# A planned hybrid-layer kernel on one core: room behind GpSimd operations and for landing remainders, and token copies spread over weight slots

## The chip, the cores and the metric

The kernel runs on one core of a Trainium2 chip. The metric is the device time of one execution in microseconds; the time of a version is the median of its runs. Within the core TensorE (PE) multiplies, VectorE (DVE), ScalarE (ACT) and GpSimd (POOL) do elementwise work, and SyncE (SP) and GpSimd issue DMAs. GpSimd's DMAs can add to what lies at their destination.

## The reference, cut to what matters

One layer for 1024 tokens of width 1024, all in f32:

```python
mod = silu(c) @ mod_w + mod_b;  shift, scale, gate = split(mod, 3)
h = rmsnorm(x, norm_g) * (1 + scale) + shift
u = h @ w_in                                   # 1024 x 5120
cv, cg, cs, lx, ls = split(u, 5)
v = cv * sigmoid(cg)
v = causal_depthwise_conv(v, dw_w, dw_b)       # 31 taps
v = silu(layernorm(v, cln_g, cln_b)) @ pw2_w + pw2_b
y_conv = v * silu(cs)
xs = causal_depthwise_conv(lx, sc_w, sc_b)     # 4 taps
r, i = sigmoid(xs @ wr + br), sigmoid(xs @ wi + bi)   # 8 heads, blocks of 128
a = exp(-8 * r * softplus(-lam))
hs = linear_scan(a, sqrt(1 - a * a) * (i * xs))
y_lru = hs * silu(ls)
y = concat([y_conv, y_lru]) @ w_out            # 2048 x 1024
out = rmsnorm(x + (1 + gate) * y, final_g)
```

## The kernel before, in words

**Tiles.** Everything is held with channels on the 128 partitions and 1024 tokens along the free dimension, so an activation of 1024 channels is eight tiles of 128x1024. `w_in` is taken in 40 blocks of 128 output channels, `pw2` in eight, `w_out` in sixteen. A block with its 1024 input channels is a *weight slot*: one DMA on SP into `raw`, a cast on ScalarE to the high part `whi`, and the low part `wlo` = `raw` - `whi`. Activations are split alike (`uh`, `ul`; `xsh`, `xsl`; `yh`, `yl`). A product in this split form takes three matmul terms (hi x hi, hi x lo, lo x hi), so a slot of eight input tiles and two halves of 512 tokens is 48 matmuls of 128x128 by 128x512 into one PSUM tile, `ps`. Three PSUM tiles of 128x1024 (`mm`) take turns and two of 128x512 (`acc`) beside them.

**The low part has three ways.** `SUB` on VectorE, `SUB` on GpSimd, or `remainder()`: ScalarE writes the negated high part and a GpSimd DMA adds the full weight from DRAM onto it. Which slot takes which is set in `weights()` by numbers (`EARLYD`, `EARLY`, `LATE`), and for the activations by similar names (`YDMA`, `LRV`, `DENG`).

**What is done with a block.** Products of `w_in` leave PSUM by ScalarE and VectorE (`evac_in`). A pair cv, cg gives `v`, and `conv_tile` runs its 31 taps: some as VectorE multiply-adds into `cacc` and `caccs`, some as ScalarE products `cq`, `co` that GpSimd DMAs add to `es` and `oo`. for an lru block `evac_in` also makes `xs` of four taps and splits it; `gates(i, n)` multiplies it by two 128x128 blocks (tile names `gate1_0` and `gate1_1` are the two halves, one for r and one for i, of head 1), takes sigmoids on ScalarE, and goes on to the scan and to `yh`, `yl`. `gate_mod` makes the output gate by eight VectorE dots per part over streamed rows of `mod_w` (tile `modw`).

**Pairs (duo).** `duo(s0, s1, n)` computes two weight blocks together. On four of the eight input tiles it needs seven products in place of eight: sums of the weight blocks (`wsh`, `wsl`, made from `wz`) times sums of the tokens (`hhs`, `hls`, made from `hx` by `token_sums` on GpSimd). Its products, called quarters, go into two PSUM tiles, `dn` and `up`; between them ScalarE copies a half of `dn` to `up` and one to the SBUF tile `wk`. The copies and the adds have priority `n + FORKN`. `lru_pair` does the same with the second half of `w_out` (tiles `lx`, `ly`, `lp`; tokens `yh`, `yl`, `yr`).

**The end.** `x_copy(m)` copies a tile of the tokens within DRAM to `accd`; GpSimd DMAs add the layer's two results to it (`acc_store`), and it is read back as `fin` for the last norm.

**What sets the order.** All calls only record operations in `class Plan`. Each has an engine, an estimated cost, a priority (about the number of the slot that it belongs to) and what it reads and writes. `order()` walks a clock: whenever an engine is free it takes, of the operations whose inputs are done and whose buffers are free, the one with the lowest priority. The list that comes out is the program: each engine executes its part strictly in that order and waits at the head of its line. So any number in the table of constants may move rows on every engine. After an operation ends, the ones that depend on it may start a latency later; for SP's DMAs that is `LANDING`, and GpSimd's adding DMAs have a `flight`. Operations of VectorE and GpSimd on SBUF are planned so that they exclude one another. `ORDER` is the order of weight slots: `i24` is block 24 of `w_in`, `g1` the gates of head 1, `i36+i28` a pair. `after_start(n)` hangs single tasks on the start of slot n: `token_sums` at `TSETS`, and all eight `x_copy` at `XCN`.

Of the kernel before, what the change touches and what calls it, by code (L numbers as in the profile page):

```python
# [14 lines left out]
P = 128  # L15
D = 1024
T = 1024
# [17 lines left out]
ORDER = "i10 i24 g0 i2 i25 i11 i3 i26 i33 i12 i4 g1 i34 i23 g2 i13 i35 i5 i27 i21 g3 i14 i19 i6 i36+i28 i15 i30+i37 i7 i29+i38 g4 g6 g5 i31 i39 i22+i18 g7 i20"  # L35
# [5 lines left out]
SPARE = 3  # L41
# [6 lines left out]
HRES = 0  # L48
# [31 lines left out]
SPILL = (0, 2, 4, 6)  # L80
SPP0, SPP1, SPN = 30, 40.5, 41
EVN = 4
CQR = 0
YHEADS, YSLOT = 2, 37
# [4 lines left out]
KQ = -0.3  # L89
TSETS = 15  # L90
DUOA = 2
# [3 lines left out]
TSP = 24  # L95
# [3 lines left out]
DENG = {14: ("DMA", "DVE", "DVE"), 15: ("POOL", "DMA", "DVE"), 16: ("DMA", "DVE", "POOL"), 17: ("DMA", "DVE", "DMA"), 18: ("POOL", "POOL", "DMA"), 19: ("DVE", "DVE", "POOL"), 20: ("POOL", "DVE", "POOL"), 21: ("DMA", "DMA", "POOL"), 22: ("DVE", "DVE", "DVE"), 23: ("POOL", "DVE", "POOL"), 24: ("POOL", "DVE", "DMA"), 25: ("POOL", "POOL", "DMA"), 26: ("POOL", "POOL", "POOL"), 27: ("POOL", "DMA", "POOL"), 28: ("POOL", "POOL", "DVE"), 29: ("DMA", "DVE", "DVE"), 30: ("DVE", "DVE", "DVE"), 32: ("POOL", "POOL", "POOL"), 34: ("DMA", "DVE", "DVE"), 35: ("DVE", "DVE", "DMA"), 36: ("POOL", "DMA", "DMA"), 37: ("POOL", "DVE", "DVE"), 38: ("DVE", "DVE", "DVE"), 39: ("DMA", "DVE", "DMA"), 40: ("DMA", "DMA", "DVE"), 41: ("DMA", "DMA", "POOL")}  # L99
YDMA = (3, 6, 7)  # L100
EVD = 0
DUOE = 1.2
# [4 lines left out]
LTP = -0.5  # L107
# [6 lines left out]
PREP, XCP = 18, 19  # L114
PLAND = 6.0
XCN = 35
# [12 lines left out]
FORKN = -3.0  # L129
# [5 lines left out]
LSN = 1  # L135
LEVN = 0.7
# [7 lines left out]
LRV = (0, 2, 4)  # L144
# [5 lines left out]
LANDING, MARGIN = 4.0, 2.0  # L150
# [7 lines left out]
EARLY = 18  # L158
EARLYD = (14, 28, 30, 31, 32, 33, 38, 40)
LATE, LAND = 41, 6.0  # L160
# [32 lines left out]
class Plan:  # L193
# [61 lines left out]
    def order(self):  # L255
# [19 lines left out]
        def done(o, end):  # L275
# [119 lines left out]
def hymba_layer(ctx: ExitStack, tc: tile.TileContext, xT, vecs, mod_w, w_first, w_in,  # L395
# [67 lines left out]
    def TT(prio, eng, out, a, b, op, n=T, r=(), w=(), reserve=0, after=()):  # L463
        e = dve if eng == "DVE" else pool
        return S.op(eng, d_cost(n) if eng == "DVE" else p_cost(n),
                    lambda: e.tensor_tensor(out=out(), in0=a(), in1=b(), op=op), prio, r, w,  # L466
                    reserve=reserve, lock=not in_psum(r), after=after)
# [91 lines left out]
    def remainder(prio, lo, hi, src, n, rk, wk, sk=(), reserve=0, after=()):  # L559
        ACT(prio, lo, lambda: hi().bitcast(F32), AF.Copy, n, scale=-1.0, r=rk, w=wk, reserve=reserve,  # L560
            after=after)
        ADD(prio, lo, src, n, r=[*wk, *sk], w=wk, flight=LAND)
# [22 lines left out]
    def weights(s, after=(), n=None, eng=None, where=None, late=(), later=()):  # L585
        n = number[s] if n is None else n
        eng = eng or ("DMA" if n in EARLYD or n >= LATE else "POOL" if n < EARLY else "DVE")
# [626 lines left out]
    def conv_pooled(i, pr, ci, vi, src, wts, every):  # L1214
# [4 lines left out]

        def product(to, z, r, x, key, scale, bias=None):  # L1220
# [4 lines left out]
        for r in range(16):  # L1225
# [5 lines left out]
            if r:  # L1231
                adds.append(ADD(pr, part(es, r, T), part(q, r, T), r=[es, q], w=[es]))
# [6 lines left out]
            if r:  # L1239
                adds.append(ADD(pr, part(oo, r, H), part(q, z * H + r, z * H + H), H,  # L1240
                                r=[(oo, 0), (q, z)], w=[(oo, 0)]))
# [44 lines left out]
    def evac_in(m, ps, n, b=None, rb=(), ev=0.5):  # L1286
# [18 lines left out]
        else:  # L1305
# [10 lines left out]
            split(pr + 0.2, xh, xl, xs)  # L1316
            lru[i] = (xs, xh, xl)

    def gates(i, n):
# [15 lines left out]
        TT(pr, "DVE", xs, g, xs, ALU.mult, r=[g, xs], w=[xs])  # L1335
# [4 lines left out]
        TT(pr, "DVE", xs, xs, r, ALU.mult, r=[xs, r], w=[xs])  # L1340
# [4 lines left out]
        TT(pr, "DVE", t, t, r, ALU.mult, r=[t, r], w=[t])  # L1345
# [10 lines left out]
        else:  # L1356
            o = split(p, yh[i], yl[i], t, reserve=SPARE)
# [63 lines left out]
    def x_copy(m, after):  # L1421
        acc_d[m] = dram.tile([P, T], F32, tag=f"acc{m}", name=f"accd{m}")
        if m:
            DMA(XCP, lambda: acc_d[m], lambda: xT[m * P:(m + 1) * P, :], FULL_BYTES, w=[("accd", m)],
                after=after)
        else:
            for z in (0, 1):
                DMA(XCP, lambda z=z: acc_d[m][:, z * H:z * H + H],
                    lambda z=z: xT[z * P // 2:(z + 1) * P // 2, :].rearrange("r (h f) -> (r h) f", h=2),
                    FULL_BYTES // 2, w=[("accd", m)], after=after)  # L1430
# [196 lines left out]
    def duo(m0, m1, n):  # L1627
# [60 lines left out]
        quarter(0.0, "A11", "B11", dn, 0, True)  # L1688
# [51 lines left out]
    def after_start(n):  # L1740
# [8 lines left out]
        if n == XCN:  # L1749
            for i in range(KT):  # L1750
                x_copy(i, [started[n]])
# [291 lines left out]
```

## Time and profile before

| | us |
|---|---|
| runs | 728.71, 729.03, 728.3 (median 728.71) |
| profiled execution | 728.47 |
| its span, first to last instruction | 726.0 |
| PE busy | 713.5 (98%), 3244 matmuls |
| VectorE busy | 655.7 (90%) |
| ScalarE busy | 474.7 (65%) |
| GpSimd busy | 206.1 (28%) |
| mean granted clock of TensorE | 0.994 |

The profiled execution takes 2.47 us more than its span, the time around the first and last instruction. A row of a timeline gives start, duration, engine, line, operation, the tile written and the tiles read (numbers left out), the shapes, a count of alike neighbours, and in brackets the idle time ahead and what ended it. The durations of neighbouring matmuls overlap, so the distance from start to start counts, not the duration.

### The profile page before, as it was taken

What the parts mean: (1) busy time and instruction counts of PE and PEld (TensorE: products, weight loads), DVE (VectorE), ACT (ScalarE), POOL (GpSimd) and SP (SyncE); (2) the same over time, 40 slices, a digit from 0 to 9 for tenths busy, and PEclk for the clock granted to TensorE, in tenths of its full rate; (3) what the DMA queues carried; (4) which work ended last, traced back from release to release, by engine and by line L of the source; (5) the groups of instructions that cost most, each with busy time, mean ns of one, the idle gap of its engine ahead of it and who ended that gap; (6) DMA issues with size and microseconds to landing.
All of it is one profiled execution on the core that took longest, in us unless ns stands there. A gap on an engine that the chain in (4) does not pass through costs nothing.

```text
span 726.0 us, 9074 instructions
## 1 busy us (share of the span) xinstructions
PE 713.5 (98%) x3244; PEld 593.0 (82%) x3244; DVE 655.7 (90%) x898; ACT 474.7 (65%) x601; POOL 206.1 (28%) x181
## 2 busy tenths in 40 slices
PE   9999999999989999999999999999999999999996
PEld 8888888888868888888888887878888888888885
DVE  7999999999988989989999999997798966999647
ACT  7650689657659974774676788846797635745322
POOL 0036334433955643075150230011101001100001
PEclk9999999999999999999999999999999999999998
DMA  8946438988788999868743466697947766774006
GB/s 335 407 157 191 65 98 227 233 249 202 179 188 215 240 220 219 216 174 172 169 109 76 152 210 177 221 311 199 259 87 156 185 151 136 234 187 178 30 1 232
DMA packets 44909, 135.17 MB, mean 186 GB/s; under 512 B 5073, under 2 KB 14545, under 8 KB 44753
## 3 DMA queue, kind: packets, MB, share of 16 engines
q1 hardware_dynamic: 27152, 88.95, 34.8%
q0 software_dynamic: 16704, 44.73, 34.4%
q10 hardware_dynamic: 1008, 0.92, 0.4%
q8 instruction: 25, 0.41, 0.2%
q14 instruction: 20, 0.16, 0.1%
HBM read 83.43 MB, written 25.17 MB: 150 GB/s over the span
## 4 chain that ended last, share of the span: by engine, by line
PE 76%; DVE 16%; issue 3%; ACT 3%; DMA 1%; DVEq 0%; POOL 0%; ACTq 0%; POOLq 0%
PE ps L599 25%; PE xout L775 6%; PE xpw L775 6%; PE first L908 5%; DVE caccs L458 5%; PE dn L1678 3%; PE up L599 3%; PE ypw L775 3%; PE lx L1478 3%; DVE xs L458 2%; PE dn L599 2%; DVE cacc L458 2%; PE gate L1329 2%; PE zout L775 1%; PE zpw L775 1%
## 5 line engine op out<-in xcount | busy, mean ns | idle before, releaser
L599 PE MATMUL ps<-uh,whi 128*128 128x512 f32 x448 | 139.1, 392 | 3.6 <-ACT r L447 3.6
L599 PE MATMUL ps<-uh,wlo 128*128 128x512 f32 x448 | 138.4, 390 | 0.0
L599 PE MATMUL ps<-ul,whi 128*128 128x512 f32 x448 | 138.3, 390 | 0.0
L599 PEld LDWEIGHTS ps<-uh,whi 128*128 128x128 f32 x448 | 84.3, 189 | 21.7 <-ACT r L447 4.0
L599 PEld LDWEIGHTS ps<-ul,whi 128*128 128x128 f32 x448 | 84.5, 189 | 17.7
L599 PEld LDWEIGHTS ps<-uh,wlo 128*128 128x128 f32 x448 | 84.4, 188 | 17.6
L439 ACT CAST whi<-raw 128x1024 fp32r<-128x1024 f32 (+1 forms) x44 | 44.3, 1011 | 39.0 <-PE ps L599 15.4
L466 POOL TENSOR_TENSOR wlo<-raw,whi 128x1024 fp32r<-128x1024 f32 (+1 forms) x17 | 44.5, 2628 | 81.4 <-ACT whi L439 81.0
L458 DVE SCALAR_TENSOR_TENSOR cacc<-v,V,cacc 128x511 f32<-128x511 f32 (+14 forms) x90 | 66.8, 743 | 0.8 <-ACT cacc L447 0.5
L458 DVE SCALAR_TENSOR_TENSOR caccs<-v,V,caccs 128x511 f32<-128x511 f32 (+6 forms) x84 | 62.5, 745 | 1.1
L458 DVE SCALAR_TENSOR_TENSOR caccs<-c,wsum,caccs 128x511 f32<-128x511 f32 (+6 forms) x84 | 62.4, 743 | 0.7
L447 ACT ACT_TABLE_LOAD x45 | 57.7, 1283 | 1.7 <-PEq L2035 0.7
L471 POOL DMA_DIRECT2D es<-cq x30 | 30.6, 1030 | 27.9 <-DMA es<-cq 9.1
L458 DVE SCALAR_TENSOR_TENSOR modw<-modw,sc 128x1024 f32<-128x1024 f32 x23 | 37.0, 1611 | 0.0
L471 POOL DMA_DIRECT2D oo<-co x26 | 25.5, 982 | 34.6 <-ACT co L447 12.3
L447 ACT ACTIVATE finsq<-fin 128x512 f32<-128x512 f32 (+2 forms) x14 | 7.9, 570 | 28.7 <-DVE fin L458 15.5
L466 DVE TENSOR_TENSOR wlo<-raw,whi 128x1024 fp32r<-128x1024 f32 (+1 forms) x19 | 23.9, 1259 | 1.2 <-ACT whi L439 1.1
L466 POOL TENSOR_TENSOR o<-fin,bc 128x256 f32<-128x256 f32 (+1 forms) x6 | 4.9, 833 | 70.4 <-ACT bc L439 70.4
L447 ACT ACTIVATE co<-v,V 128x510 f32<-128x510 f32 (+12 forms) x26 | 18.1, 711 | 5.9 <-DVE modw L458 3.6
L471 POOL DMA_DIRECT2D lz<-in_w_out_dram x16 | 14.2, 960 | 26.2 <-ACT lz L447 24.2
L447 ACT ACTIVATE cq<-v,V 128x511 f32<-128x511 f32 (+14 forms) x30 | 21.3, 709 | 0.0
L471 POOL DMA_DIRECT2D accd<-acc x8 | 7.3, 914 | 48.0 <-ACT acc L447 29.1
(515 smaller groups left out, 1926.4 us busy)
## 6 DMA issues: line engine op xcount, KB each, us to landing
raw<-in_w_in_dram SPq DMA_DIRECT2D x36, 512.0 KB, 4.8
modw<-in_mod_w_dram SPq DMA_DIRECT2D x24, 512.0 KB, 7.8
scsd<-scs SPq DMA_DIRECT2D x8, 512.0 KB, 3.4
raw<-in_w_out_dram SPq DMA_DIRECT2D x8, 512.0 KB, 5.9
accd<-acc POOLq DMA_DIRECT2D x8, 512.0 KB, 6.4
rawpw<-in_pw_dram SPq DMA_DIRECT2D x8, 512.0 KB, 4.4
scsr<-scsd SPq DMA_DIRECT2D x8, 512.0 KB, 5.0
rawout<-in_w_out_dram SPq DMA_DIRECT2D x8, 512.0 KB, 3.4
```

The source lines that it names most:

```text
L439: act.copy(out(), in_())
L447: act.activation(out=out(), in_=in_(), func=func, **kw)
L458: dve.scalar_tensor_tensor(out=out(), in0=in0(), scalar=scalar, in1=in1(), op0=op0, op1=op1, accum_out=accum)
L466: lambda: e.tensor_tensor(out=out(), in0=a(), in1=b(), op=op), prio, r, w,
L471: return S.op("POOL", ISSUE, lambda: pool.dma_start(out(), a(), accum_op=ALU.add), prio, r, w, lag=RATE * n / T, after=after, flight=flight)
L599: pe.matmul(ps()[:, a - off:b - off], k3(lhs)()[:, at, :], rhs[k]()[:, a:b], start=(k == first and lhs is wh and rhs is xh and (a - off) % ...
L775: pe.matmul(half(ps, 0)(), half(*lhs)()[:, j * P:j * P + P], half(*rhs)(), start=start and at == 0 and i == 0, stop=at == len(order) - 1 a ...
L908: pe.matmul(ps()[:, a - off:b - off], fw_part(lhs, k, i * P, i * P + P)(), rhs()[:, a:b], start=k == 0 and lhs is wh and rhs is xh, stop=k ...
L1329: pe.matmul(ps()[:, c0:c1], lhs()[:, j, :], rhs()[:, c0:c1], start=st == 0, stop=st == 2)
L1478: pe.matmul(half(ps, h)(), lhs()[:, o:o + P], half(*rhs)(), start=begin and at == 0 and t == 0, stop=at == len(order) - 1 and t == len(ter ...
L1678: pe.matmul(half(ps, h)(), lhs()[:, o:o + P], half(rhs, z)(), start=begin and j == 0 and t == 0, stop=j == NJ - 1 and t == 2, skip_group_c ...
```

## The change

The code computes the same with the same four pairs of slots, now paired 28 with 37 and 36 with 30 instead of 36 with 28 and 30 with 37. The planner's numbers differ:

- every GpSimd operation that isn't a DMA has 1.5 us more latency to its dependents (`PLAG`), `LANDING` is 4.5 for all of SP's loads, and adding DMAs are planned with 8 us of flight (`LAND`) in place of 6;
- `ORDER` is another order of slots and gates; pairs start their preparation at other priorities (`DUOA`, `KQ`), their copies at `FORKN` -200, ahead of anything else;
- tables say which engine makes which low part (`WE`), and which products of the lru path go to GpSimd (`PGM`, `PXR`, `PYM`, `PXL`, `PYL`); fewer pairs have an engine of their own in `DENG`;
- `x_copy(m)` hangs on slot 28 + m each, with twice the planned duration, instead of all eight on slot 35.

```diff
-ORDER = "i10 i24 g0 i2 i25 i11 i3 i26 i33 i12 i4 g1 i34 i23 g2 i13 i35 i5 i27 i21 g3 i14 i19 i6 i36+i28 i15 i30+i37 i7 i29+i38 g4 g6 g5 i31 i39 i22+i18 g7 i20"
+ORDER = "i10 i24 i2 g0 i25 i11 i3 i26 i12 i33 i4 g1 i34 i23 g2 i13 i35 i5 i27 g3 i21 i39 i14 i6 i28+i37 i15 i36+i30 i7 g4 i29+i38 g5 g6 i31 i19 i22+i18 i20 g7"
-KQ = -0.3
+KQ = 0.5
-DUOA = 2
+DUOA = 3
-TSP = 24
+TSP = 30
-DENG = {14: ("DMA", "DVE", "DVE"), ...
+DENG = {27: ("POOL", "DMA", "POOL"), 30: ("DVE", "DVE", "DVE")}
-YDMA = (3, 6, 7)
+YDMA = (1, 4, 6, 7)
-XCN = 35
+XCN = 28
+XCS = 1
-FORKN = -3.0
+FORKN = -200
-LRV = (0, 2, 4)
+LRV = (0, 1, 2, 3, 4, 6)
-LANDING, MARGIN = 4.0, 2.0
+PLAG, PSLOW = 1.5, 1.0
+LANDING, MARGIN = 4.5, 2.0
-EARLY = 18
-EARLYD = (14, 28, 30, 31, 32, 33, 38, 40)
-LATE, LAND = 41, 6.0
+EARLY = 20
+WE = {6: "DMA", 7: "DVE", 14: "DMA", 18: "DVE", 19: "DVE", 25: "POOL", 32: "DMA", 39: "DMA"}
+PGM, PYM, PXL, PYL, PXR = (2, 3, 7), (4,), (5,), (1, 4, 5, 6, 7), (4, 6)
+LATE, LAND = 41, 8.0
...
                 if o.eng == "SP" and o.prio > 0:
-                    lat = LANDING if o.prio < 37 else 3.0
+                    lat = LANDING
+                if o.eng == "POOL" and not o.lag:
+                    lat += PLAG
...
-        TT(pr, "DVE", xs, g, xs, ALU.mult, r=[g, xs], w=[xs])
+        TT(pr, "POOL" if i in PGM else "DVE", xs, g, xs, ALU.mult, r=[g, xs], w=[xs])
...
-            DMA(XCP, lambda: acc_d[m], lambda: xT[m * P:(m + 1) * P, :], FULL_BYTES, w=[("accd", m)],
+            DMA(XCP, lambda: acc_d[m], lambda: xT[m * P:(m + 1) * P, :], 2 * FULL_BYTES, w=[("accd", m)],
...
-        if n == XCN:
-            for i in range(KT):
-                x_copy(i, [started[n]])
+        if 0 <= (n - XCN) // XCS < KT and (n - XCN) % XCS == 0:
+            x_copy((n - XCN) // XCS, [started[n]])
```

By the rows of the two programs, both issue the same matmuls; VectorE issues nine instructions fewer and GpSimd nine more. Three places:

TensorE around the second gate, before: the last rows of `ps16`, the gate's two halves, then `ps17`.

```order
L599 MATMUL ps16_1735<-uh7_487,whi16_1660 128x512 x2
L599 MATMUL ps16_1735<-ul7_506,whi16_1660 128x512 x2
L599 MATMUL ps16_1735<-uh7_487,wlo16_1684 128x512 x2
L1329 MATMUL gate1_0_1819<-xsh1_1372,ghi1_592 128x512 x2
L1329 MATMUL gate1_0_1819<-xsl1_1383,ghi1_592 128x512 x2
L1329 MATMUL gate1_0_1819<-xsh1_1372,glo1_995 128x512 x2
L1329 MATMUL gate1_1_1831<-xsh1_1372,ghi1_592 128x512 x2
L1329 MATMUL gate1_1_1831<-xsl1_1383,ghi1_592 128x512 x2
L1329 MATMUL gate1_1_1831<-xsh1_1372,glo1_995 128x512 x2
L599 MATMUL ps17_1841<-uh0_189,whi17_1743 128x512 x2
```

TensorE at the same place now:

```order
L606 MATMUL ps16_1754<-uh7_487,whi16_1675 128x512 x2
L606 MATMUL ps16_1754<-ul7_506,whi16_1675 128x512 x2
L606 MATMUL ps16_1754<-uh7_487,wlo16_1701 128x512 x2
L1341 MATMUL gate1_1_1833<-xsh1_1384,ghi1_602 128x512 x2
L1341 MATMUL gate1_1_1833<-xsl1_1397,ghi1_602 128x512 x2
L1341 MATMUL gate1_1_1833<-xsh1_1384,glo1_983 128x512 x2
L606 MATMUL ps17_1849<-uh0_189,whi17_1761 128x512 x2
```

The half `gate1_0` now stands 75 rows earlier, between `ps13` and `ps14`.

GpSimd at that time before: token sums (`hx`), weight remainders (`wlo`) and conv sums (`es`, `oo`, as DMAs).

```order
L466 TENSOR_TENSOR hx00_1671<-uh0_189,ul0_206 128x1024
L466 TENSOR_TENSOR wlo16_1684<-raw16_1491,whi16_1660 128x1024
L466 TENSOR_TENSOR hx01_1699<-uh1_230,ul1_243 128x1024
L466 TENSOR_TENSOR hx00_1671<-hx00_1671 128x512
L471 DMA es1_1050<-cq1_6_1619 128x1018
L466 TENSOR_TENSOR hx00_1671<-hx01_1699,hx00_1671 128x512
L466 TENSOR_TENSOR wlo17_1756<-raw17_1599,whi17_1743 128x1024
L466 TENSOR_TENSOR hx01_1699<-hx01_1699,hx00_1671 128x512
```

GpSimd from the same sum on, now:

```order
L473 TENSOR_TENSOR hx00_1687<-uh0_189,ul0_206 128x1024
L473 TENSOR_TENSOR wlo16_1701<-raw16_1495,whi16_1675 128x1024
L473 TENSOR_TENSOR hx00_1687<-hx00_1687 128x512
L478 DMA es1_1028<-cq1_7_1626 128x1017
L478 DMA oo1_1043<-co1_6_1544 128x505
L478 DMA es3_1518<-cq3_1_1531 128x1023
L478 DMA oo3_1522<-co3_2_1556 128x509
L473 TENSOR_TENSOR wlo17_1766<-raw17_1606,whi17_1761 128x1024
L478 DMA es1_1028<-cq1_8_1711 128x1016
L478 DMA oo1_1043<-co1_8_1720 128x504
L478 DMA es3_1518<-cq3_2_1547 128x1022
```

The sums `hx01` moved behind these rows; conv sums stand between.

TensorE in the pair that begins with slot 27, before, from its second quarter (the first is the six rows ahead):

```order
L1678 MATMUL dn27_2754<-hhs00_1767,wsh27_2733 128x512
L1678 MATMUL dn27_2754<-hls00_1816,wsh27_2733 128x512
L1678 MATMUL dn27_2754<-hhs00_1767,wsl27_2746 128x512
L1678 MATMUL dn27_2754<-hhs10_2097,wsh27_2733 128x512
L1678 MATMUL dn27_2754<-hls10_2118,wsh27_2733 128x512
L1678 MATMUL dn27_2754<-hhs10_2097,wsl27_2746 128x512
L599 MATMUL ps29_2781<-uh0_189,whi29_2758 128x512 x2
L599 MATMUL ps29_2781<-ul0_206,whi29_2758 128x512 x2
L599 MATMUL ps29_2781<-uh0_189,wlo29_2767 128x512 x2
L1678 MATMUL up27_2788<-uh1_230,whi27_2678 128x512
L1678 MATMUL up27_2788<-ul1_243,whi27_2678 128x512
L1678 MATMUL up27_2788<-uh1_230,wlo27_2697 128x512
```

TensorE there now, from the end of the first quarter:

```order
L1690 MATMUL dn27_2755<-uh2_275,whi27_2671 128x512
L1690 MATMUL dn27_2755<-ul2_284,whi27_2671 128x512
L1690 MATMUL dn27_2755<-uh2_275,wlo27_2686 128x512
L1690 MATMUL up27_2769<-uh1_230,whi27_2671 128x512
L1690 MATMUL up27_2769<-ul1_243,whi27_2671 128x512
L1690 MATMUL up27_2769<-uh1_230,wlo27_2686 128x512
L1690 MATMUL up27_2769<-uh3_322,whi27_2671 128x512
L1690 MATMUL up27_2769<-ul3_331,whi27_2671 128x512
L1690 MATMUL up27_2769<-uh3_322,wlo27_2686 128x512
```

The `up` products now follow the first quarter of `dn` directly; the second quarter and the rows of `ps29` moved behind them.

More of the change, by code (lines that the diff above doesn't have):

```diff
@@ L586, in weights @@
         n = number[s] if n is None else n
-        eng = eng or ("DMA" if n in EARLYD or n >= LATE else "POOL" if n < EARLY else "DVE")
+        eng = eng or WE.get(n) or ("DMA" if n >= LATE else "POOL" if n < EARLY else "DVE")
         w_bufs(s, where)
@@ L1356, in gates @@
         else:
-            o = split(p, yh[i], yl[i], t, reserve=SPARE)
+            o = split(p, yh[i], yl[i], t, eng="POOL" if i in PYL else "DVE", reserve=SPARE)
         if i < YHEADS and i not in YSP:
```

49 lines of the change are left out of this document (27 added, 22 removed).

## The prediction

> **What bounds the kernel now.** I read the page's busy times first, then busy time by windows, then TensorE's waits, and last the timelines around each wait.
>
> ```profile
> span 726.0 us, 9074 instructions
> PE 713.5 (98%) x3244; PEld 593.0 (82%) x3244; DVE 655.7 (90%) x898; ACT 474.7 (65%) x601; POOL 206.1 (28%) x181
> 50.00:200.00 150.00, 150.00 (x670) 124.28 (x669) 148.62 (x223) 96.49 (x128) 74.28 (x60) 1.00 0.71 176
> 200.00:250.00 50.00, 46.43 (x199) 37.96 (x198) 44.56 (x48) 40.78 (x47) 30.21 (x23) 0.97 0.90 212
> 300.00:400.00 100.00, 100.00 (x442) 82.78 (x442) 95.45 (x120) 70.65 (x84) 39.11 (x33) 1.00 0.61 144
> 409.00:416.00 7.00, 7.00 (x32) 5.81 (x31) 7.00 (x6) 3.50 (x5) 3.51 (x3) 1.00 0.93 318
> 410.00:450.00 40.00, 39.80 (x175) 32.25 (x174) 39.96 (x45) 30.45 (x30) 11.29 (x8) 1.00 0.71 209
> 450.00:500.00 50.00, 49.26 (x218) 40.47 (x217) 45.33 (x55) 31.83 (x37) 6.16 (x7) 1.00 0.82 251
> 500.00:700.00 200.00, 199.99 (x903) 165.70 (x902) 162.56 (x217) 122.31 (x161) 20.16 (x23) 1.00 0.61 156
> ```
>
> The window rows give the window, its length, then busy time and count of PE, PEld, DVE, ACT and POOL, the granted clock, the DMA share and GB/s. TensorE is the bound: from 300 to 400 us it runs 442 matmuls in 100 us without a hole, 0.226 us each. The change leaves every matmul in, so it can only take back what TensorE loses between them. VectorE is nearly as full: 148.62 of 150 us, and 39.96 of 40. The waits say where TensorE loses:
>
> ```profile
> PE ps L599 <- ACT r L447: 3.6, 1, 3.6
> PE ly L599 <- DMA wlo<-in_w_out_dram: 0.7, 1, 0.7
> PE dn L1678 <- ACT wk L439: 0.2, 1, 0.2
> ```
>
> **Term 1: the pause at the second gate, -5.4 us.** On TensorE:
>
> ```profile
> 203.94 0.61 PE L1329 MATMUL gate<-xsh,glo 128*128 128x512 f32 x2
> 208.12 1.17 PE L599 MATMUL ps<-uh,whi 128*128 128x512 f32 x2 [3.57 <-ACT r L447]
> 211.64 0.62 PE L599 MATMUL ps<-ul,whi 128*128 128x512 f32 x2
> ```
>
> Two matmuls from 203.94 should make room for the next at 204.40; it starts at 208.12, 3.72 late. The eight from 208.12 to 211.64 take 3.52 instead of 8 x 0.226 = 1.81, another 1.71: the window 200 to 250 has a mean clock of 0.97. Together 5.43. Behind it stand ScalarE and VectorE:
>
> ```profile
> 205.07 1.05 ACT L439 CAST hhs<-hx 128x1024 fp32r<-128x1024 f32 x1 [9.99 <-DVE modw L458]
> 206.97 1.11 ACT L447 ACTIVATE r<-gate,V 128x1024 f32<-128x1024 f32 x1
> 187.59 5.24 DVE L458 SCALAR_TENSOR_TENSOR modw<-modw,sc 128x1024 f32<-128x1024 f32 x1
> 200.29 4.69 DVE L458 SCALAR_TENSOR_TENSOR modw<-modw,sc 128x1024 f32<-128x1024 f32 x1
> L458 DVE SCALAR_TENSOR_TENSOR modw<-modw,sc x23: 1195/1218/5242, 9.5 to 308.3; 128x1024 f32<-128x1024 f32 x23
> 183.03 2.75 POOL L466 TENSOR_TENSOR hx<-uh,ul 128x1024 f32<-128x1024 f32 x1
> ```
>
> The last gate row of TensorE needs ScalarE's activation of its result before the PSUM tile is free for ps17, and that activation stands on ScalarE behind a cast which had sat idle 9.99 us for VectorE's modw dot. Two such dots took 5.24 and 4.69 us where the median is 1.22 (7.49 too long), while GpSimd ran token sums, 2.75 us each at full width, back to back. In the new order the first half of this gate stands 75 rows earlier on TensorE, so the tile that ps17 takes was freed by an older product, and GpSimd's sums are spread out with DMA issues between them. What can be late next is a conv product on ScalarE behind the same kind of dot; nothing of TensorE's next rows hangs on it. I take the whole 5.43; the other end is 0, if an equal pause comes back.
>
> **Term 2: remainder of weight 41, -1.0 us.**
>
> ```profile
> 484.21 0.39 PE L599 MATMUL ly<-yl,whi 128*128 128x512 f32 x1
> 485.33 0.50 PE L599 MATMUL ly<-yh,wlo 128*128 128x512 f32 x1 [0.74 <-DMA wlo<-in_w_out_dram]
> 485.67 0.39 PE L1478 MATMUL lx<-yls,lsh 128*128 128x512 f32 x1
> ```
>
> From 484.21 to 485.67 pass 1.46 us for two intervals of 0.226: 1.01 lost, the only loss that I find in this window. The remainder was one of GpSimd's accumulating DMAs; now VectorE subtracts it. VectorE has 4.7 us free in 450 to 500, and its nearest row of that size (below, v, 1.22) fits in. This also takes one issue off GpSimd's queue ahead of the accd stores, and a copy of the negated high part off ScalarE. Ends: -1.0, or 0 if VectorE comes to it late.
>
> **Term 3: duo 37, -0.5 us.**
>
> ```profile
> 441.88 0.59 ACT L439 COPY wk<-dn 128x512 f32<-128x512 f32 x1 [0.74 <-DVE r L1341]
> 441.93 0.39 PE L1678 MATMUL up<-uh,wlo 128*128 128x512 f32 x1
> 442.52 0.50 PE L1678 MATMUL dn<-hhs,wsh 128*128 128x512 f32 x1 [0.20 <-ACT wk L439]
> 442.86 0.40 PE L1678 MATMUL dn<-hls,wsh 128*128 128x512 f32 x1
> ```
>
> From 441.93 to 442.86 pass 0.93 us for two intervals: 0.48 lost. A later quarter of dn overwrote what ScalarE had yet to copy to wk. Now all of dn's quarters up to there come first and the up products afterwards, so up's copy has six more matmuls, 1.36 us, against the 0.59 of such a copy. Ends -0.5 and +0.5 (up's copy now stands behind a cast).
>
> **Term 4: fifth gate, -0.3 us.**
>
> ```profile
> 419.44 0.61 PE L1329 MATMUL gate<-xsh,ghi 128*128 128x512 f32 x2
> 420.60 0.63 PE L1329 MATMUL gate<-xsh,glo 128*128 128x512 f32 x2
> 418.22 1.76 DVE L466 TENSOR_TENSOR xsl<-xs,xsh 128x1024 fp32r<-128x1024 f32 x1
> L466 POOL TENSOR_TENSOR wlo<-raw,whi 128x1024 fp32r<-128x1024 f32 (+1 forms) x17 | 44.5, 2628 | 81.4 <-ACT whi L439 81.0
> ```
>
> From 419.44 to 420.60 pass 1.16 us for four intervals (0.90): 0.26 lost to the subtraction xsl, which ends on VectorE at 419.98. It goes to GpSimd, whose subtractions take 2.63 us, 0.87 more, but which sits idle there (11.29 busy of 40). It can start when ScalarE's cast is done and not when VectorE's line allows. Ends -0.3 and +0.6; I take -0.3.
>
> **Term 5: duo 27, +0.9 us.** This is a new wait. The up products followed dn's first two quarters and six matmuls of ps29; they now follow the first quarter at once. They accumulate onto a copy that ScalarE makes of that quarter. The chain is the last matmul's 0.39, the copy's 0.59 and the 0.05 from a copy's end at 442.47 to the matmul at 442.52: 1.03 against 0.23 between neighbours, so 0.80, and the 0.11 that the second interval after such a pause was long (0.34 against 0.226): 0.91. Ends: 0, if it stays hidden as before, and 2.0 if the copy queues behind one activation of 1.1 us (the r row above).
>
> **Term 6: VectorE early on, +0.6 us.**
>
> ```profile
> L458 DVE SCALAR_TENSOR_TENSOR fsum<-raw,shift,fsum x21: 334/348/2474, 59.6 to 84.6; 128x128 f32<-128x128 f32 x21
> 87.21 0.71 PE L599 MATMUL ps<-uh,whi 128*128 128x512 f32 x2
> 124.12 1.22 DVE L466 TENSOR_TENSOR v<-ps,sig 128x1024 f32<-128x1024 f32 x1
> 125.40 0.73 PE L599 MATMUL ps<-uh,whi 128*128 128x512 f32 x2
> ```
>
> The seven bias sums move ahead of 18 matmuls, 4.1 us. Their last input starts at 84.6 and takes 0.35 (done at 84.95), and they end at 87.2, so some 2.2 us were free and 1.9 are missing. VectorE has one product of 0.75 fewer before them, and of the early weights GpSimd subtracts two fewer, which should take back at least the 2.13 by which one sum was stretched: covered by 1 us. The second place is ps10: v ends at 125.34, the matmul starts at 125.40, nothing to spare. More VectorE work now stands ahead of v relative to TensorE (up to 2.4 us by counting rows), less the stretching that goes away. Ends 0 and 2.4; I take 0.6, near the lower end since VectorE starts that stretch earlier.
>
> **Term 7: nothing from the token copies, +0.6 for the rest.**
>
> ```profile
> L485 SPq DMA_DIRECT2D accd<-in_xT_dram x9: 489/589/657, 409.3 to 414.8; - x9
> DMA to landing us min/median/max: 3.4/7.1/12.8
> L485 SPq DMA_DIRECT2D raw<-in_w_in_dram x36: 327/328/765, 28.9 to 421.7; - x36
> ```
>
> Nine copies within DRAM leave in a burst from 409.3; the DMA share goes to 0.93, and TensorE is busy 7.00 of 7.00, so the burst cost it nothing (the 410 to 450 window's hole is terms 3 and 4). Spread over slots 28 to 35, one each 48 matmuls or 10.9 us, each lands (7.1 median over all accd DMAs, with the stores) before the next. On SP's in-order queue each stands ahead of a weight load. Cover: weights are loaded 2.5 slots ahead. Across seven hundred microseconds of moved rows I add 0.6, the size of terms 3 and 4 as the nearest rows for small waits that I did not find. The nine elementwise operations that go to GpSimd (xs by the gates, one sls, one xsl, one yl) take about 9 x 1.2 us off VectorE; off TensorE's path they count zero.
>
> **Sum.** 728.47 (profiled; 2.5 around the span) - 5.4 - 1.0 - 0.5 - 0.3 + 0.9 + 0.6 + 0.6 = 723.4. The median of the runs, 728.71, is 0.24 above the profiled one: 723.6.
>
> **Rivals.**
> *A: the order holds as planned (faster still).* No wait at duo 27 or early: without terms 5 to 7, 721.5. Against it: the copy's 0.59 us is longer than two matmuls.
>
> *B: VectorE behind GpSimd (no change).* Nine more operations of 2.63 us on GpSimd are 23.7 us. Were VectorE held for all of that, it would lose 23.7 and save 11. The measured share is smaller: 7.49 us of stretching in two dots, over the 22 us from 183.03 to the second one's end at 204.98, is 0.34 us per us, so 8 lost against 11 saved. Where VectorE has no room (39.96 of 40) three of them, xsl, yl and one gate product, would cost 7.9 - 3.7 = 4.2 us at the full share: 727.8. [...] One more pause of term 1's kind, 5.4, gives 729.0 and ends the same. That price holds for a long pause only: after the 0.74 us wait at 485.33 the clock stayed at 1.00. [...]
>
> *C: early VectorE (less gain).* The bias sums late by the missing 1.9 and ps10 by another 1.4: 726.9. For it: VectorE's 148.62 of 150.
>
> *D: the token copies hold up weight loads (slower).* A copy takes SP's queue 0.59 us instead of 0.33, and at its longest landing, 12.8 us, fills more than a slot of 10.9. If a weight load behind it lands over the lead late, ScalarE's cast waits at the head of its line and TensorE pauses as at 204: 5.4 each time. One leaves 729.0; from two on, 734.4, it decides. Against it: the burst of nine, with a weight load behind it at 421.7, made no wait.
>
> **Chances and range.** Forecast 0.50 (722.2 to 725.2), A 0.11, C 0.15, B 0.13, D 0.11. About 0.2%, 1.5 us, can be told from no change here. Faster: forecast, A, C: 0.76. Within: B, 0.13. Slower: D, 0.11. From A's end, less 0.5 for the tail, to the upper part of B, 721.0 to 728.4, holds 0.84; a narrower one would lose C or B.
>
> **What would show it.** TensorE's waits without "ACT r" and without "DMA wlo"; a mean clock of 1.00 between 200 and 250; a new wait of "up" on ACT of 0.8 us near 318; gate rows of the fifth gate 0.45 us apart. VectorE's sum some 10 us lower and GpSimd's some 20 higher. I am wrong if a pause above 3 us stands anywhere with the clock at 0.5 behind it, if "raw" appears as a releaser of ScalarE's casts with TensorE waiting behind, or if TensorE's waits before 130 us pass 2 us.

## The result: slower, 737.2 us

Four runs of the changed kernel gave 736.92 to 738.74, median 737.2; four of the kernel before beside them 728.5. The ratio is 1.0124, with an interval of 1.0106 to 1.0141: 8.7 us slower, where 5 us faster was forecast. The profiled execution took 738.74, 1.5 above the median, so its pauses may be a little longer than the typical ones.

The page's first lines and busy time by windows, in the columns explained above:

```profile
span 737.0 us, 9085 instructions
PE 717.2 (97%) x3244; PEld 594.7 (81%) x3244; DVE 652.2 (88%) x889; ACT 477.7 (65%) x604; POOL 223.2 (30%) x190
200.00:250.00 50.00, 48.28 (x213) 39.66 (x212) 45.81 (x50) 32.66 (x37) 29.46 (x19) 1.00 0.78 196
270.00:300.00 30.00, 24.93 (x99) 19.84 (x98) 29.72 (x38) 14.66 (x18) 10.72 (x11) 0.89 0.96 217
410.00:450.00 40.00, 39.34 (x173) 31.93 (x172) 39.36 (x40) 33.51 (x33) 19.02 (x14) 1.00 0.44 118
450.00:500.00 50.00, 47.63 (x204) 38.93 (x202) 45.53 (x57) 35.42 (x37) 8.20 (x6) 0.97 0.87 263
500.00:700.00 200.00, 199.96 (x895) 164.74 (x894) 166.10 (x220) 121.67 (x161) 21.00 (x24) 1.00 0.60 152
```

TensorE's holes have moved: the worst is now 270 to 300, where it was busy 24.93 of 30 us at a mean clock of 0.89. TensorE's waits name what ended them (three at the very start and end of the kernel, and one of 0.2 us, are left out):

```profile
PE gate L1341 <- DVE xsl L473: 4.4, 2, 3.9
PE dn L1690 <- DVE up L473: 2.4, 1, 2.4
PE ps L606 <- ACT scs L454: 1.7, 1, 1.7
PE gate L1341 <- ACT xsh L446: 1.1, 1, 1.1
PE up L1690 <- ACT up L446: 0.7, 1, 0.7
```

`xsl` and `xsh` are the two parts of `xs` that a gate multiplies, `scs` is what ScalarE writes when it takes a cs block out of its PSUM tile, and `up` and `dn` are a duo's two tiles. Neither "ACT r" nor "DMA wlo" stands there any more. What took their place, in TensorE's timeline:

```profile
228.55 0.61 PE L1341 MATMUL gate<-xsh,glo 128*128 128x512 f32 x2
230.88 0.73 PE L606 MATMUL ps<-uh,whi 128*128 128x512 f32 x2 [1.72 <-ACT scs L454]
...
286.35 0.61 PE L606 MATMUL ps<-uh,wlo 128*128 128x512 f32 x2
288.10 0.73 PE L1341 MATMUL gate<-xsh,ghi 128*128 128x512 f32 x2 [1.14 <-ACT xsh L446]
292.77 1.22 PE L1341 MATMUL gate<-xsl,ghi 128*128 128x512 f32 x2 [3.93 <-DVE xsl L473]
...
297.82 0.40 PE L606 MATMUL ps<-ul,whi 128*128 128x512 f32 x1
...
454.23 0.61 PE L1341 MATMUL gate<-xsh,glo 128*128 128x512 f32 x2
457.21 0.50 PE L1690 MATMUL dn<-hhs,wsh 128*128 128x512 f32 x1 [2.37 <-DVE up L473]
```

From start to start against 0.226 us a matmul, TensorE loses 2.0 us after the third gate, 7.9 at the fourth (1.3 + 4.2 waiting, 2.3 in the twelve matmuls from 292.77 to 297.82, most at the half clock: the granted clock was 0.5 from 290.7 to 297.5), 1.0 at duo 27, 1.2 around gate seven and duo 37, and 4.3 at duo 37's second part (2.5 waiting, the rest at the half clock, 0.5 from 457.96 to 461.37). That is 16.4 where the kernel before lost 7.2. Of the 1.8 that are left of the 11.0 us between the two spans, 1.2 lie behind 715 us, in the waits for the last norm (`finbc`) and after the last matmul.

### The profile page after: what moved, and what is told of

Same layout as the page of the kernel before. It is cut to its first block, busy times and chain, and to the rows that moved or that the text cites. A ratio compares the mean times of both kernels' runs of the same rounds, so it can differ in the third digit from the quotient of the medians.

```text
span 737.0 us, 9085 instructions
## 1 busy us (share of the span) xinstructions
PE 717.2 (97%) x3244; PEld 594.7 (81%) x3244; DVE 652.2 (88%) x889; ACT 477.7 (65%) x604; POOL 223.2 (30%) x190
## 4 chain that ended last, share of the span: by engine, by line
PE 76%; DVE 16%; issue 4%; ACT 2%; DMA 1%; POOL 0%; DVEq 0%; ACTq 0%
PE ps L606 26%; PE xout L782 6%; PE xpw L782 6%; PE first L915 5%; DVE caccs L465 3%; PE lx L1490 3%; PE ypw L782 3%; PE dn L1690 2%; PE dn L606 2%; DVE modw L465 2%; PE up L606 2%; PE gate L1341 2%; PE zpw L782 1%; PE zout L782 1%; PE lx L606 1%
## 5 line engine op out<-in xcount | busy, mean ns | idle before, releaser
L465 DVE SCALAR_TENSOR_TENSOR modw<-modw,sc 128x1024 f32<-128x1024 f32 x23 | 35.0, 1520 | 0.0
L473 DVE TENSOR_TENSOR wlo<-raw,whi 128x1024 fp32r<-128x1024 f32 (+1 forms) x20 | 26.5, 1326 | 4.0 <-ACT whi L446 4.0
L1353 DVE TENSOR_TENSOR_SCAN r<-a,xs 128x1024 f32<-128x1024 f32 x8 | 20.9, 2616 | 0.1
```

Of the source, the lines that this page charges most:

```text
L465: dve.scalar_tensor_tensor(out=out(), in0=in0(), scalar=scalar, in1=in1(), op0=op0, op1=op1, accum_out=accum)
L1353: S.op("DVE", 2.2, lambda: dve.tensor_tensor_scan(out=r(), data0=a(), data1=xs(), initial=0.0, op0=ALU.mult, op1=ALU.add), pr, [a, xs], [r])
```

## The experiments

An edit of "one row" below is made behind the planner: its list is kept, a named row is put elsewhere on its own engine's line, and the lists are merged again so that every row still follows what it depends on. No other engine's order changes; the buffers that rows write are assigned anew.

### Two parts alone on the kernel before: b_r1 and b_copies

b_r1, on ScalarE:

```diff
+r1 <- gate1_0
 hhs01 <- hx01
 whi18 <- raw18
-r1 <- gate1_0
```

> The kernel before, with one instruction of ScalarE moved: the activation of the second gate's first half (r1) now stands ahead of the cast hhs01 that waits for VectorE's dot, and ahead of the cast of weight 18; nothing else differs. Theory P (term 1 of the prediction: the pause is a fault of the order on ScalarE and its 5.4 us are to be had): 728.5 - 5.4 = 723.1, up to 724. Theory Q (VectorE is the second bound, its window 50 to 200 is 99% full; the pause at 204 was the place where TensorE waited off VectorE's arrears, and without it TensorE comes 5 us earlier to products of VectorE that are no earlier): TensorE waits for VectorE or ScalarE again before 300 us, by 1.4 to 4 us, and the time is 725.5 to 728.5.

Measured 726.27 (ratio 0.9972, 0.9959 to 0.9984): 2.0 of 5.4 us. TensorE's wait for r1 is gone, and a new one stands 24 us later, with a half clock behind it (0.5 for 3.41 us):

```profile
PE ps L634 <- ACT scs L482: 2.3, 1, 2.3
228.47 0.61 PE L1364 MATMUL gate<-xsh,glo 128*128 128x512 f32 x2
231.40 0.95 PE L634 MATMUL ps<-uh,whi 128*128 128x512 f32 x2 [2.32 <-ACT scs L482]
```

It is the place where the changed kernel waits too. Theory Q held: the pause passes on, and the time lies in the range that it gave.

b_copies takes the change's `XCN = 28`, one copy a slot, without the doubled planned duration:

> The kernel before, with the copies of the tokens hung one on each slot from 28 on; nine DMA rows of SP move, no row of another engine. Theory P (copies hidden either way): 728.5 within 0.7. Rival D of the prediction (a copy ahead of a weight load makes the load late): a wait of TensorE behind a cast of a raw weight and 731 or more.

Measured 728.33, ratio 1.0003 (0.9989 to 1.0017). The spread of the copies costs and brings nothing that shows within 1.2 us, and no wait of the changed kernel names a copy or a landing of `raw`. Rival D is out.

### One row at each of the long pauses: a_xsl3 and a_up37

On VectorE in the changed kernel:

```diff
+xsl3 <- xs3,xsh3
 gate1 <- macc,b1
 caccs4, cacc5, caccs4, cacc5 (taps)
-xsl3 <- xs3,xsh3
```

> The changed kernel, with one instruction of VectorE moved: the low part xsl3 stands five rows earlier, ahead of gate1's scale and four taps. The wait of TensorE at the fourth gate was 1.3 us for the cast xsh, 4.1 for xsl3, 0.4 after the waits, and 1.8 in ten matmuls at the half clock. If the position on VectorE's line is the cause (xsl3 starts when the cast ends, at 288.05, and ends at 289.3, 0.8 after TensorE wants it), the long pause and the half clock go: 737.2 - 5.1 = 732.1, up to 733. If VectorE as a whole is behind, the taps that now come later make the next waits longer (gate seven, duo 37, 445 to 460 us) by as much as was won: 735 to 737.

Measured 735.99, 1.2 us of the 5.1. The loss at the fourth gate shrank to 0.4 us, and another took its place:

```profile
PE up L1725 <- ACT up L481: 5.0, 1, 5.0
```

At duo 27 TensorE now waited 5 us for ScalarE's copy, which stood behind a cast (wsh27) that waited for GpSimd. The second reading above, that the arrears go on (the work by which VectorE's and ScalarE's lines are behind), held, though at another place than it named.

> The changed kernel, with one instruction of VectorE moved: the add into up37 stands seven rows earlier, ahead of seven taps. It could start when ScalarE's copy to wk ends, 453.23, and end at 453.9, before TensorE wants it at 454.7. If the line position is the cause, the wait of 2.5 us, 0.1 after it and 1.8 at the half clock go: 737.2 - 4.4 = 732.8, up to 733.6. If something else holds TensorE there (the copy to wk, or the gate's PSUM tile), less than half of it goes: 735 or more.

Measured 735.03, 2.2 us of the 4.4: the wait of 2.4 for up37 went, and 1.3 us came up at the next product of that duo (dn37, for VectorE's second add).

### The source of the arrears: a_zero and a_zero3

```diff
-x = uh + ul; differences of halves; hls = x - hhs      # 16 operations, GpSimd
+memset(..., 0.0) of the same tiles                     # a_zero once, a_zero3 three times
```

> The changed kernel, in its order row for row, but GpSimd's sixteen token-sum operations write zeros (no operand is read, a shorter write), so the products with token sums are left out of the result. In the changed kernel VectorE's instructions are 16.4 us longer in all than their like between 200 and 300 us (6.5 before), while GpSimd makes these sums. Theory S (GpSimd's sums are the source of the arrears: they stretch VectorE's instructions, and ScalarE's casts wait for them): VectorE's stretching in 200 to 300 falls below 6, the waits at the third and fourth gate (2.0 and 7.6 us) go to less than 2 together: 737.2 - 8 = 729, down to 725 if duo 37's goes too. Theory O (the order gives VectorE more rows ahead of what TensorE wants than it can do, sums or not): both waits stay to two thirds and more: 734 to 737.

> As a_zero (the changed kernel, products with token sums left out of the result), with every write of zeros done three times, so that GpSimd is busy about as long as with the sums (a write of 128x1024 took 0.95 to 1.3 us, a sum 2.4 to 2.7) and ScalarE's casts wait for it as long. Theory S1 (the stretching of VectorE's instructions by GpSimd's sums makes the arrears; writes of zeros don't stretch them): 726 to 728, as a_zero. Theory S2 (GpSimd's length makes them: ScalarE's casts wait at the head of its line for GpSimd, whoever stretches): the pauses at the third and fourth gate come back, 732 to 737.

Both leave the products with token sums out of the result. a_zero took 726.08 (ratio to the kernel before 0.9982, 0.9971 to 0.9994), a_zero3 727.54 (0.9991, 0.9981 to 1.0002). The two medians differ by 1.5 us, the profiled executions (725.91 and 725.97) do not; what the 1.5 is wasn't looked into. The window 200 to 300 us of the changed kernel, of a_zero and of a_zero3:

```profile
200.00:300.00 100.00, 93.21 (x399) 76.06 (x398) 91.82 (x100) 61.71 (x74) 55.98 (x39) 0.97 0.86 207
200.00:300.00 100.00, 100.00 (x443) 82.78 (x442) 83.92 (x108) 71.57 (x85) 37.88 (x41) 1.00 0.88 215
200.00:300.00 100.00, 100.00 (x443) 82.84 (x442) 83.69 (x109) 71.26 (x84) 58.81 (x69) 1.00 0.88 216
```

The columns are TensorE, its weight loads, VectorE, ScalarE and GpSimd. Same program rows, but without the sums VectorE does eight instructions more in 8 us less, and TensorE has no hole. In a_zero3 GpSimd is busy 58.81 us, longer than with the sums (55.98), and in the trace nothing changes for the others. So it is not GpSimd's length, nor ScalarE's casts waiting for it, but what its two-input sums do to VectorE's instructions. In the changed kernel these lie on the rows that the gates need, or ahead of them. Two such rows, each with what GpSimd ran beside it:

```profile
268.29 3.77 DVE L465 SCALAR_TENSOR_TENSOR modw<-modw,sc 128x1024 f32<-128x1024 f32 x1
268.25 2.71 POOL L473 TENSOR_TENSOR hls<-hx,hhs 128x1024 fp32r<-128x1024 f32 x1
289.52 3.19 DVE L473 TENSOR_TENSOR xsl<-xs,xsh 128x1024 fp32r<-128x1024 f32 x1
289.08 2.54 POOL L473 TENSOR_TENSOR wlo<-raw,whi 128x1024 fp32r<-128x1024 f32 x1
```

The median dot takes 1.22, an undisturbed xsl 1.22. Adding up, for every VectorE instruction, what it took above its like (the median of the same operation and shape), the changed kernel has 16.4 us of stretching between 200 and 300 us, the kernel before 6.5, and a_zero not 0.3. (xsl3 was stretched by a weight's subtraction, not a token sum; a_zero is on time there because what comes ahead is.)

### Moving rows at all pauses: a_fix, a_zero_fix

```diff
 ScalarE: scs7 one row ahead, before a cast of a token sum (hhs)
 VectorE: modw19 7 rows ahead, xsl3 5, xsl7 1, up37 7
 TensorE: dn27's second quarter ahead of up27's products
```

> The changed kernel with seven rows moved at the five places where TensorE waits: scs7 one row ahead on ScalarE and the dot modw19 seven rows on VectorE (third gate), xsl3 five rows (fourth), dn27's second quarter back ahead of up27's products on TensorE, xsl7 one row and up37's add seven rows on VectorE. If each pause is a fault of its own place: 737.2 - 2.0 - 5.1 - 1.0 - 0.7 - 4.4 = 724.0. If arrears of VectorE and ScalarE move on to the next place: a new pause of over 1 us somewhere in 228 to 460, and 727 to 733.

Measured 740.01, slower than the changed kernel:

```profile
PE gate L1376 <- ACT xsh L481: 3.9, 1, 3.9
PE dn L1725 <- ACT up L481: 3.4, 2, 2.5
PE dn L1725 <- POOL wsl L508: 1.1, 1, 1.1
```

xsl3 no longer held the fourth gate, xsh3 did, as late. At duo 27 the second quarter waited for the same copy "up" as up27's products had, so my reading of that order was wrong too: here the second quarter waits for the copy although it writes dn's other half.

> As a_zero, with the local moves of a_fix at the pauses that a_zero has left: up37's add seven rows ahead, xsl7 one, dn27's second quarter ahead of up27's products. a_fix, with the arrears, was slower by these and other moves. If moves of rows pay in full where VectorE and ScalarE are not in arrears: 726.1 - 2.6 - 1.0 - 0.7 = 721.8, to 723. If the pauses just move on here too: 725 to 727.

Measured 725.83 against 726.08: nothing that shows. Here too the waits went on within the two duos (0.9 at dn27, 1.1 and 1.3 at dn37). Moves by hand at the point of a pause didn't pay even without arrears, against what I expected.

### The kernel before, without sums and with the sums elsewhere: b_zero, b_sums_dve, b_hls_dma

> The kernel before, row for row, with GpSimd's sixteen token sums replaced by writes of zeros as in a_zero (products with token sums left out of the result). If the sums cost the kernel before as much as the changed one (11 us), 717; but TensorE has only 7.2 us of pauses there, so 721.5 is the floor. Theory U (the sums hurt both kernels, and the changed order is no better without them): the pause at 204 goes, 722 to 724, under the 726.1 of a_zero. Theory V (the change moved the sums to a worse place and is otherwise an improvement): 726 to 728.

Measured 722.63 (ratio 0.9916, 0.9901 to 0.9931). The pause at 204 is gone and none of its kind follows. So the sums cost the kernel before 5.8 us and the changed one 11.1 (737.2 - 726.1). Of the 8.7 us between the two, about 5.3 go with the sums' worse places, and 3.5 (726.1 - 722.6) are there without any sums. In the two traces most of these 3.5 are waits around duo 27 and duo 37: 4.7 us in a_zero, while b_zero loses 1.7 at the places of terms 2 to 4. What makes the waits around duo 37 wasn't tried.

> The kernel before, planned with the sixteen token sums on VectorE in place of GpSimd; the planner moves rows from slot 16 on. VectorE gets about 8 x 1.2 + 8 x 0.7 = 15 us more work and loses the stretching (13 us between 183 and 210 and after), and no cast of ScalarE waits for GpSimd. If the stretching is the whole price of GpSimd's sums: 724 to 729, with no instruction of VectorE stretched by over 1 us between 170 and 300. If VectorE has no room for the work itself: 732 or more.

Measured 743.54: in 200 to 300 no VectorE instruction is stretched, but the work itself has no room: TensorE waits at nine places for 0.7 to 3.4 us, the longest in the lru pairs.

> The kernel before, planned with the four low parts of the token sums (hls) made by ScalarE's negated copy and an adding DMA in place of GpSimd's subtraction: 4 two-input operations of 2.4 to 3.4 us fewer on GpSimd, 4 x 1.1 us more on ScalarE, rows moved from slot 17 on. If fewer two-input sums mean less stretching: the pause at 204 or its successor shrinks by up to 3 us, 724 to 727. If ScalarE's line pays for it (it is full around 211 to 232): 729 to 734.

Measured 744.8. ScalarE pays, as the second reading has it, and more than it said: waits for ScalarE's "up" copy (2.9) and cast "whi" (2.3), and for a landing (2.8).

### The room alone and all but the room: b_room, a_room0

```diff
-lat = LANDING if o.prio < 37 else 3.0
+lat = LANDING                       # 4.5
+if o.eng == "POOL" and not o.lag:
+    lat += PLAG                     # 1.5; LAND, PLAND 8
```

> The kernel before, planned with the room alone: 1.5 us of latency behind GpSimd's operations, 4.5 behind SP's loads, 8 us of flight for adding DMAs; slot order, engines and copies as before. The planner moves rows on all engines. Theory O (slot order and engines make the new pauses): 726 to 730. If the room itself does it (the plan holds rows back for landings, and TensorE's waits come from rows planned too late): 732 or more.

Measured 734.41 (ratio 1.0089, 1.0065 to 1.0114). In the profiled execution (737.17, the longest of the four) two waits make most of it, each with a half clock behind it (the mean granted clock of the span is 0.989, against 0.994 in the kernel before): 2.7 us for scs at the same third gate, 2.6 for a weight's landing in the lru pairs. This trace also shows what moved the token sums. The second full-width sum on GpSimd's line, in the changed kernel, in b_room and in the kernel before:

```profile
204.56 2.72 POOL L473 TENSOR_TENSOR hx<-uh,ul 128x1024 f32<-128x1024 f32 x1
206.61 2.72 POOL L504 TENSOR_TENSOR hx<-uh,ul 128x1024 f32<-128x1024 f32 x1
187.76 2.73 POOL L466 TENSOR_TENSOR hx<-uh,ul 128x1024 f32<-128x1024 f32 x1
```

In the changed kernel and in b_room 14 of the 16 sums start behind 200 us, in the kernel before 10. Counted as above, b_room's VectorE has some 16 us of stretching between 200 and 300 us, like the changed kernel's, against some 7 in the kernel before. So the planner's room, with the old slot order and engines, is enough to put the sums where they stretch these rows; which of its numbers does it wasn't tried. The 1.0 us at duo 27 is lost in b_room too.

> The changed kernel, planned without the room (no latency behind GpSimd, 4.0 behind SP's loads, 6 us of flight), with its slot order, engines and copies. The planner moves rows on all engines. The room alone on the kernel before gave 734.4. If the room is the part that makes the change slower: 727 to 730. If the slot order and the tables of engines, which were made together with the room, need it: 735 or more.

Measured 805.67: waits of 11.2, 10.7, 5.7 us and many smaller ones. The changed slot order was made with the room and is far worse without it, so the 8.7 us can't be shared out between the room and the rest.

### Towards a faster version: b_fix, b_fix2, b_r1_w41, b_v4, b_v4_x

> The kernel before with r1 ahead on ScalarE as in the first experiment, scs7 five rows ahead on ScalarE (the next pause there: 2.5 us, 0.1, and 1.8 at the half clock), and the low part of weight 41 subtracted by VectorE in place of an adding DMA (1.0 us). If the pauses are faults of their places: 726.3 - 4.2 - 1.0 = 721.1, to 722. If arrears move on: another pause before 300 us, and 723 to 726.

Measured 727.86: scs7's pause is gone and one of 1.4 + 3.3 us, with 1.7 lost at the half clock behind it, stands at the fourth gate, where the kernel before had none. Three fixed places, nothing gained.

> The second experiment on the kernel before (r1, scs7, wlo41), with xsh3 three rows ahead on ScalarE and xsl3 eight rows on VectorE, at the fourth gate, where the pause had moved (1.4 + 3.3 + 0.4 us and 1.7 at the half clock). If this was its last place: 727.9 - 6.4 = 721.5, to 723. If the arrears move on again: 724 to 728, with a pause in 300 to 460.

Measured 731.6. VectorE's line, with xsl3 early, stood still in front of it:

```profile
284.96 0.74 DVE L493 SCALAR_TENSOR_TENSOR caccs<-v,V,caccs 128x501 f32<-128x501 f32 x1
291.89 1.23 DVE L501 TENSOR_TENSOR xsl<-xs,xsh 128x1024 fp32r<-128x1024 f32 x1 [6.20 <-DMA oo<-co]
```

By the profile the row waited for a conv sum's adding DMA, not for its operand xsh3, which was done at 286.2.

> The kernel before with r1 ahead on ScalarE and the low part of weight 41 on VectorE, without the other moves. The pause at 229 stays (4.3 us with its half clock), the wait for the remainder at 484 (1.0) goes, and nothing upstream of the fourth gate is changed against the first experiment: 726.3 - 1.0 = 725.3. If arrears also move the pause at 484 on: 726 to 727.

Measured 725.92 (ratio 0.9964, 0.9951 to 0.9977): the wait at 484 is gone, and the time fell by some 0.4 us against b_r1's, inside the scatter of runs.

b_v4 goes upstream of the pause at 229. On VectorE:

```diff
+v4 <- ps16,sig4
 wlo18 <- raw18,whi18
-v4 <- ps16,sig4
```

> The kernel of b_r1_w41 with VectorE's v4 one row earlier, ahead of the low part of weight 18 (which waits 2.4 us for ScalarE's cast and is then stretched from 1.2 to 2.5 by GpSimd's sum). ScalarE waited 3.5 us for v4 behind it, and its line was full from there to the pause at 229 (2.5 us and 1.8 at the half clock). If the source is hit: that pause shrinks below 0.5 us. If the arrears end with it: 725.9 - 4.2 = 721.7. If they come out at the fourth gate, as in b_fix (1.4 + 3.3 + 2.1 there): 725 to 728.

Measured 724.29 (ratio 0.9942, 0.9926 to 0.9958), the profiled execution 723.0. ScalarE's g1, in b_r1 and in b_v4:

```profile
210.50 1.12 ACT L482 ACTIVATE g<-gate,V 128x1024 f32<-128x1024 f32 x1 [3.48 <-DVE v L501]
206.35 1.12 ACT L482 ACTIVATE g<-gate,V 128x1024 f32<-128x1024 f32 x1
```

What follows it on ScalarE comes 3 to 4 us earlier, scs7 too (226.93 against 230.34), and between 200 and 300 TensorE has no hole:

```profile
200.00:300.00 100.00, 100.00 (x442) 82.61 (x441) 94.49 (x118) 77.38 (x92) 47.30 (x40) 1.00 0.96 228
PE dn L1713 <- ACT wk L474: 0.2, 1, 0.2
```

That last row is the only wait that the view names between 5 and 710 us. The fourth gate didn't wait: the arrears had ended. This version beats both, by 3.9 us and 12.9.

> As b_v4, with xsh3 one row ahead on ScalarE (before the cast of a weight) and xsl3 five rows on VectorE at the fourth gate. In b_fix xsh3 ran at 289.1 and xsl3 at 292.8, TensorE wanted them at 288.8 and 289.3; with the moves they come at 287.8 and 289.1 (ends 288.8 and 290.3), a wait of 1.0 and no half clock: 722 to 723.5. If VectorE or ScalarE stand behind something else there (adding DMAs that free ScalarE's buffers, as in b_fix2): 726 to 729.

Measured 727.32. The two added moves, which forestalled a pause that wasn't there any more, made one: 2.0 us for xsl at the fourth gate and 1.2 at duo 27.

## Why the prediction was wrong, by its own steps

- **Terms 1 to 4** were right as to the places: all four pauses (7.2 us) are gone in the trace after. At duo 37 the other end that term 3 allowed came in: of the 1.2 us there, some 0.5 are TensorE waiting for the copy to `up`. What was wrong was to count term 1 as gained. Of its 5.4, b_r1 kept 2.0. I had called the other end "0, if an equal pause comes back" and named a conv product on ScalarE on which "nothing of TensorE's next rows hangs"; but two weights later TensorE does hang on ScalarE's line, at scs7, and that line was late by the same chain. In b_v4, where the row that starts the chain is moved and not only the one at which TensorE waits, TensorE waits for nothing between 200 and 300 us; the median, with weight 41 moved as well, fell by 3.9 us.
- **Term 5**, duo 27, was priced at 0.91 and measured 0.98.
- **Term 6**, VectorE early, was priced at 0.6: TensorE waits for nothing between 60 and 228 us in the trace after. VectorE's stretching did shrink there, as the term says: 7 us before 200 us, against 17 in the kernel before.
- **Term 7 is the step that failed**: "nothing from the token copies, +0.6 for the rest". The copies cost nothing (b_copies), but the rest was 15.4 us: pauses at the third gate, the fourth gate and duo 37's second part, 14.2 us in all, of which the prediction named none, and the 1.2 around gate seven and duo 37. It asked at each place that it knew how much time was spare in the trace before, with VectorE's stretching there unchanged or less, and term 1 read "GpSimd's sums are spread out" as a relief. Spread out, the sums run later, beside other rows. The changed plan brings the fourth gate to TensorE 7.4 us earlier (286.8 against 294.15): 18 fewer matmuls stand ahead of it, 4.1 us, and the rest is the pause that is gone at the second gate, less the new one at the third. VectorE does not come earlier by as much: with 16.4 us of stretching in 200 to 300 against 6.5, xsl3 ends at 292.7 where it had ended at 293.2. The rows of the kernel before:

```profile
294.15 0.62 PE L1329 MATMUL gate<-xsh,ghi 128*128 128x512 f32 x2
292.02 1.22 DVE L466 TENSOR_TENSOR xsl<-xs,xsh 128x1024 fp32r<-128x1024 f32 x1
```

  There xsl3 had 1.4 us to spare (the gate's first two matmuls don't need it); no term of the prediction asked what becomes of them.
- **Rival B**, with 0.13 and 727.8 to 729.0, had the kind of mechanism, VectorE held by GpSimd, but the wrong rows and the wrong size. It charged the nine operations that are new on GpSimd; no stretched row between 200 and 300 us stands beside one of them, they stand beside the token sums and weight subtractions that GpSimd had before. And it cost one pause, while the stretching acts over 60 us on rows that VectorE has there with both inputs in SBUF, and arrears showed up as pauses at one place after another. The share used against it, 0.34 us of stretching per us of GpSimd work, was set off against the instructions that VectorE saved; seven of the nine lie behind 300 us, and the stretching ahead of them. **Rival A** would have needed the rest to be nothing. **C** and **D** didn't occur.
- The prediction's own sign of being wrong, a pause above 3 us with the half clock behind it, stands at the fourth gate. VectorE's busy time fell by 3.5 us (655.7 to 652.2) and not by some 10, GpSimd's rose by 17 (206.1 to 223.2) as forecast; neither sum decides anything. Over the whole span the stretching is not much more either, 32 us against 27: what changed is which rows it meets.

What put the sums over the dots and the gates' rows is the planner's room, as far as b_room's trace shows. Priorities of the sums (`TSP`) have no part in it: set back to 24, the program comes out row for row the same.

## What to carry to other kernels

When TensorE waits for a line that is itself full, moving the row at the wait can pass much of the wait on: b_r1 kept 2.0 us of 5.4, a_up37 2.2 of 4.4, a_xsl3 1.2 of 5.1, b_fix nothing, and b_fix2 lost. The one move that kept the gain, v4, was at the head of the chain, where the waiting line first stood idle (a PSUM reader behind a subtraction that had to wait). Before counting a removed pause as gained, go along the next two or three rows at which the bound engine needs the late one, with the late engine's own times. And a plan that treats two engines as excluding one another should be held against the trace by kind of instruction: what it got wrong here was less the total than the row that is late.

## What the runs showed of the hardware

**Which VectorE instructions GpSimd stretches.** One group of the kernel before's taps (minimum, median, maximum in ns), and six taps of the changed kernel with the token sum that ran beside them:

```profile
L458 DVE SCALAR_TENSOR_TENSOR caccs<-v,V,caccs x84: 734/744/754, 148.3 to 488.9; 128x511 f32<-128x511 f32 x6, 128x510 f32<-128x510 f32 x6, 128x509 f32<-128x509 f32 x6, 128x508 f32<-128x508 f32 x6
223.26 4.68 DVE L465 SCALAR_TENSOR_TENSOR cacc<-v,V,cacc 128x511 f32<-128x511 f32 x6
223.64 2.40 POOL L473 TENSOR_TENSOR hls<-hx,hhs 128x1024 fp32r<-128x1024 f32 x1 [8.52 <-ACT caccs L454]
```

No tap was stretched: of the 264 in the kernel before, 72 ran beside a two-input operation of GpSimd, 47 of them all the way, and none took more than 0.77 us. The dots, with 1.2 us median, went to 5.24. Where the operands lie told them apart here. Both inputs of a dot are tiles in SBUF; a tap adds onto `cacc` or `caccs`, which are `acc` tiles in PSUM, and reads one tile from SBUF. It held for the other rows too: dots, full-width subtractions (a wlo at 205.10 of the changed kernel took 3.27 us, its median 1.22) and products (an xs at 208.30, 2.32 against 1.22) and the small sums of `fsum` (one of 2.47 against 0.35 in the kernel before), with both inputs in SBUF, were stretched; the full-width product `v`, which reads a PSUM tile, took its 1.22 us twice in the changed kernel with such an operation beside it all the way; and of 98 instructions of the kernel before with an input in PSUM that ran beside such an operation none was, nor of the 111 in the changed kernel (at most 0.015 us above their like). With writes of zeros in place of the sums VectorE was busy 83.69 us of the 100 at 58.81 us of GpSimd (a_zero3), and 83.92 at 37.88 (a_zero), where its stretching was under 0.3.

**The half clock after a short pause.** By the granted clock in the traces, the clock fell in b_r1 to 0.5 for 3.41 us behind a pause of 2.5 us, in a_xsl3 behind one of 2.0 at 230; in the changed kernel it did so after 2.5 at 457 and did not after 1.9 at 229 (1.00 from 229 to 235), and in a_zero it did not after 2.5 at 446 (mean of the span 0.996). At the pause of 4.2 it stayed at 0.5 for 6.83 us. The prediction put the price of the half clock on a long pause only, from the wait of 0.74 us at 485.33 alone, with the clock at 1.00 after it; of the pauses of 2.0 and 2.5 us named here, three cost 1.7 us more and one nothing more.
